# The gated output weights of a hybrid mLSTM block: preparing them beside the first q projection and the last scan

## The chip, the cores and the metric

The kernel runs on one core of a Trainium2 chip. The metric is device time in microseconds (us) of the whole program, lower is better. Engines are named as in the profile: PE (TensorE matmul) and PEld (its weight load), DVE (VectorE), ACT (ScalarE), POOL (GpSimd), and SP, whose queue issues nearly all DMAs.

## The reference, cut to what matters

One encoder layer over 2048 tokens of width 1024. `c` gives six modulation vectors, and the layer has two parts:

```python
mod = silu(c) @ w_ada + b_ada
sh1, sc1, gt1, sh2, sc2, gt2 = split(mod, 6)
h = rmsnorm(x, g_mix) * (1 + sc1) + sh1
q, k, v, o, gates, u = split(h @ w_in)
y_a = sigmoid(o) * headnorm(scan_fwd(q,k,v) + scan_bwd(q,k,v))   # 4 heads, chunks of 128 tokens
y_b = pool(u) ...                                                # windows 2, 4, 8, 16
x = x + gt1 * (concat(y_a, y_b) @ w_out)
x = x + gt2 * (square(relu(h2 @ w_ff1)) @ w_ff2)                 # h2 from x, g_ffn, sh2, sc2
return rmsnorm(x, g_final)
```

`gt1 * (y @ w_out)` is computed as `y @ (w_out * gt1)`, gt1 scaling the columns of `w_out`. That product, and every later one, is made with seven half-size products in place of eight (a Strassen form), so the scaled weight is needed as four blocks and as sums of blocks.

## The kernel before, in words

All matrix work is in split 32-bit form: an operand is a high part (an ACT copy) and a low part (a DVE subtraction), and each product takes three matmuls.

The stages, in program order:

- Norm and the v and gate projections. Beside them DVE forms columns of `mod` (`mod_col`, L119 to L123): 512 KB of `w_ada` are loaded and one L117 multiplies by silu(c) (`c_bc`) and sums, one column of 128 values each.
- Pooling, groups 3 to 0: the u projection of a group, its window sums on DVE, its part of the output weights (`wo_d`) and ten or so more columns of `mod`. The last columns, 38 to 47, come in group 0.
- `qk_proj(0)`: the k blocks 3, 2, 1, 0 of head 0 and then its q blocks 0 to 3, 512 tokens and 24 matmuls each. After each k block `k_post` transposes it, scales it twice on DVE (`kb` L497, `kf` L498) and builds four states of the backward scan (PE L508, DVE L511 and L513).
- For each head the `scan` over 16 chunks, with the `qk_proj` of the next head as *fill* between its steps (after the last head the four `o_proj`). A head later than 0 has its q blocks first and its k blocks last. The fill of head h+1 first loads `wr(h+1)` and `wr(4+h+1)` (`col_weights`, L390 to L397), turns each into `wh` (ACT L395) and `wl` (DVE L396), and then multiplies (L404 to L406).
- The output product with the scaled `w_out`, and the MLP.

**Preparing the output weights.** `mod` is transposed on PE (`modT`, L694), copied by ACT (L696), written to DRAM (`mod_d`, L697), and its row gt1 is read back on all partitions (L699). The generator `out_sums` (L666 to L684) then takes four pairs of rows, k = 0 to 3. For each it loads two 512 KB rows (`os`, L671) from `w_out` and `wo_d`, multiplies each by gt1 (L674), stores three blocks (L678), makes four block differences in place (L682), and stores each (L684). A block is 256 KB. One k is eight steps of the generator: loads, two products, the stores, four differences.

**Buffers.** The tag `raw` has three buffers of 512 KB. The loads of `w_ada`, the loads `wr` of all projections and the rows `os` share it. gt1 takes the one buffer of tag `bc`, which was `c_bc`'s. `wh` and `wl` have two buffers each. The two PSUM tiles of tag `tp` serve every transpose; the three of `ev` serve the copies of q and k, `kf`, and the copy of modT.

**What sets the order.** Up to the output product, a planner writes each engine's instruction list at build time. It follows its own estimate of when operands are ready; of the instructions that are ready in that estimate the earliest in program order goes first. A tile whose tag has no free buffer waits, in program order, until the last reader of an older tile of the tag is done. Each engine, and SP's DMA queue, then executes its list in order and waits in place. `keep_in_program_order` puts an instruction behind the one that precedes it on its engine in program order.

Of the kernel before, what the change touches and what calls it, by code (L numbers as in the profile page):

```python
# [12 lines left out]
ALU = mybir.AluOpType  # L13
# [8 lines left out]
NB = T // 512  # L22
H = 4
# [12 lines left out]
def block_kernel(ctx, tc, x, x_t, cb, w_ada, b_ada, g_mix, g_ffn, g_head, p_scale, w_col, w_vg,  # L36
                 w_v2, w_o, w_1, w_2, w_pool, b_gate, edge, g_fin, out):
    nc = tc.nc
    ve, sc, gp, pe, dma = nc.vector, nc.scalar, nc.gpsimd, nc.tensor, nc.sync.dma_start
# [16 lines left out]
    def raw(name, n=D):  # L56
        t = wp.tile([P, D], F32, tag="raw", name=name, bufs=3)
        return t[:, :n]

    def evt(name):  # L60
        return wev.tile([P, 528], F32, tag="ev", name=name)
# [4 lines left out]
    def tp(name):  # L66
        return psA.tile([P, 512], F32, tag="tp", name=name)
# [322 lines left out]
    def col_weights(ci):  # L390
        r = raw(f"wr{ci}").rearrange("p (k n) -> p k n", k=KT)
        dma(r, w_col[ci])
        hh = wq.tile([P, KT, P], F32R, tag="whi", name=f"wh{ci}")
        hl = wq.tile([P, KT, P], F32R, tag="wlo", name=f"wl{ci}")
        sc.copy(hh, r)  # L395
        ve.tensor_tensor(hl, r, asf(hh), ALU.subtract)  # L396
        return hh, hl  # L397

    def col_mm(ci, b, w):

        hh, hl = w
        ps = mm(f"c{ci}_{b}")
        for k in range(KT):
            pe.matmul(ps, hh[:, k], Hh[b][:, k], start=k == 0, stop=False)  # L404
            pe.matmul(ps, hh[:, k], Hl[b][:, k], start=False, stop=False)  # L405
            pe.matmul(ps, hl[:, k], Hh[b][:, k], start=False, stop=k == KT - 1)  # L406
            if k in (2, 5, 7):
                yield
        return ps

    def mod_row(j0):
        return mod_d[j0:j0 + KT, :].rearrange("(o a) n -> o (a n)", o=1).broadcast_to([P, D])


    with tc.tile_pool(name="pu", bufs=2) as pu, tc.tile_pool(name="psU", bufs=2, space=PSUM) as psU:
# [8 lines left out]
        for g in (3, 2, 1, 0):  # L424
# [21 lines left out]
            n = T + 15  # L446
# [30 lines left out]
    with tc.tile_pool(name="ps_", bufs=2) as sp, tc.tile_pool(name="psS", bufs=1, space=PSUM) as psS:  # L477

        def qk_proj(h, C):


            def k_post(b, ps):
                vt = sp.tile([P, 4, 129], F32, tag="va", name=f"va{h}_{b}", bufs=2)
                dma(vt, v_d[b][h])
                e = evt(f"k{h}_{b}")[:, :512]
                sc.copy(e, ps)
                dma(qk_d[h][b][:, 1, :], e)
                yield
                pt = tp(f"kn{h}_{b}")
                for j in range(4):  # L490
                    pe.transpose(pt[:, j * P:(j + 1) * P], e[:, j * P:(j + 1) * P], ident)
                pt = pt.rearrange("p (c e) -> p c e", c=4)
                r0 = h * NT + 4 * b
                kf = evt(f"kf{h}_{b}")[:, :512].rearrange("p (c e) -> p c e", c=4)
                kb = sp.tile([P, 4, P], F32, tag="kb", name=f"kb{h}_{b}", bufs=1)
                r1 = r0 + 64
                ve.tensor_tensor(kb, pt, wkcol[:, r1:r1 + 4].unsqueeze(2).broadcast_to([P, 4, P]), ALU.mult)  # L497
                ve.tensor_tensor(kf, pt, wkcol[:, r0:r0 + 4].unsqueeze(2).broadcast_to([P, 4, P]), ALU.mult)  # L498
                dma(kw_d[h][b], kf)
                yield  # L500
                for j0 in (3, 1):
                    kv = psS.tile([P, 2, 256], F32, tag="kv", name=f"kvb{h}_{4 * b + j0}")
                    for j in (j0, j0 - 1):
                        c = 4 * b + j
                        if c == 0:
                            break
                        kvj = kv[:, j0 - j, 0:129]
                        pe.matmul(kvj, kb[:, j], vt[:, j], start=True, stop=True)  # L508
                        Cn = sp.tile([P, 129], F32, tag="Cb", name=f"Cb{h}_{c}", bufs=17)
                        if c == NT - 1:  # L510
                            ve.tensor_copy(Cn, kvj)  # L511
                        else:
                            ve.scalar_tensor_tensor(Cn, C[c], decb[:, r1 + j:r1 + j + 1], kvj,  # L513
                                                    ALU.mult, ALU.add)
                        C[c - 1] = Cn
                    yield

            def q_post(b, ps):
                e = evt(f"q{h}_{b}")[:, :512]
                sc.mul(e, ps, float(P) ** -0.5)  # L520
                dma(qk_d[h][b][:, 0, :], e)


            p = iter(())
            if h == 0:
                wk_, wq_ = wn, col_weights(0)
            else:
                wq_, wk_ = col_weights(h), col_weights(4 + h)
            for n in range(2 * NB):
                is_k = (n < NB) == (h == 0)  # L530
                b = NB - 1 - n % NB if is_k else n % NB
                g = col_mm(4 + h if is_k else h, b, wk_ if is_k else wq_)
                while True:
                    try:
                        next(g)
                    except StopIteration as e:
                        ps = e.value
                        break
                    next(p, None)
                    yield  # L540
                for _ in p:
                    pass
                if is_k:
                    p = k_post(b, ps)
                    next(p)
                else:
                    q_post(b, ps)
            for _ in p:
                yield
# [108 lines left out]
        def o_proj(h):  # L658
            w = col_weights(8 + h)
            for b in range(NB):  # L660
                ps = yield from col_mm(8 + h, b, w)
                e = evt(f"o{h}_{b}")[:, :512]
                sc.copy(e, ps)
                dma_act(o_d[b][:, h, :], e)

        def out_sums(gt1):  # L666

            for k in range(4):
                rows = [raw(f"os{h}_{k}") for h in range(2)]
                for h, src in enumerate((w_o[k], wo_d[k])):  # L670
                    dma(rows[h], src)  # L671
                yield
                for h in range(2):
                    ve.tensor_tensor(rows[h], rows[h], gt1, ALU.mult)  # L674
                    yield
                b11, b12, b21, b22 = [r[:, 512 * n:512 * n + 512] for r in rows for n in range(2)]
                for place, b in ((0, b11), (1, b21), (5, b22)):
                    dma(wot_d[place, :, k], b)  # L678
                yield
                for place, dst, x_, y_ in ((3, b11, b12, b11), (4, b12, b22, b12), (2, b22, b22, b11),  # L680
                                           (6, b21, b21, b22)):
                    ve.tensor_tensor(dst, x_, y_, ALU.subtract)  # L682
                    yield
                    dma(wot_d[place, :, k], dst)  # L684

        def chain(*gs):
            for g in gs:
                yield from g

        Cb = [None] * NT  # L690
        for _ in qk_proj(0, Cb):
            pass
        mt = tp("modT")
        pe.transpose(mt[0:48, 0:P], mod, ident)  # L694
        me = evt("modTe")
# [2 lines left out]
        gt1 = wp.tile([P, D], F32, tag="bc", name="gt1", bufs=1)  # L698
        dma(gt1, mod_row(16))  # L699
        osum = out_sums(gt1)  # L700
        for h in range(H):
            Cn = [None] * NT
            if h + 1 < H:
                fill = qk_proj(h + 1, Cn)
            else:
                fill = chain(*(o_proj(i) for i in range(H)))
            n = 0
            for _ in scan(h, Cb):
                n += 1
                if n % EVERY == 0:  # L710
                    next(fill, None)
                if h > 0 and n % 4 == 0:
                    next(osum, None)
            for _ in fill:
                pass
            Cb = Cn
# [554 lines left out]
```

## Time and profile before

| what | value |
|---|---|
| time, median of 3 runs | 2049.32 us (2046.41 to 2052.79) |
| the profiled execution's own time | 2054.1 us |
| its span, first to last instruction | 2052.2 us |
| mean granted TensorE clock | 0.996 of full speed |
| busy: PE, PEld, DVE, ACT, POOL | 97%, 81%, 66%, 45%, 6% of the span |

The 2052.2 us are the stretch that the views show; 1.9 us of the execution lie outside it. "Busy" counts an instruction from its start to its modelled end, so PE is busy at 97% and still has room in places; the idle time of PEld is the sharper sign. In this execution the q blocks of head 0 run from about 268 us to 291 us, the scan of head 0 with the fill of head 1 to about 375 us, those of heads 1 and 2 to about 455 and 537 us, and the last scan to about 605 us.

### The profile page before, as it was taken

The numbers are of one execution on the slowest core, as the hardware profiler recorded it, in microseconds if no ns is written. First come the engines' busy times: TensorE is split into PE (matmuls) and PEld (weight loads), VectorE is DVE, ScalarE is ACT, GpSimd is POOL, SyncE is SP. The second block draws the span as 40 slices with busy tenths as digits, with TensorE's granted clock in tenths as the row PEclk, the third lists the DMA queues.
The fourth block names the chain that finished last, engine by engine and source line by source line (L and its number), as shares of the span: only waits on it lengthen the run. The fifth ranks groups of instructions, "written<-read, shape, count | busy, mean of one in ns | idle before, by whom it ended". The sixth has DMA issues, their size and how long they took to land.

```text
span 2052.2 us, 27784 instructions
## 1 busy us (share of the span) xinstructions
PE 1991.4 (97%) x9591; PEld 1659.4 (81%) x9591; DVE 1356.0 (66%) x2456; ACT 917.9 (45%) x1704; POOL 132.0 (6%) x353
## 2 busy tenths in 40 slices
PE   7999998989999999999999999999999999999998
PEld 6887777778887877788888888888888888888886
DVE  6638646666646766555666766666877767767876
ACT  4722123333335667655556755556323324324432
POOL 1100012222210110000000000000000000000011
PEclk9999999999999999999999999999999999999999
DMA  8836866877548798655666766666877748658554
GB/s 340 232 114 216 275 198 214 255 254 225 176 141 269 234 276 282 199 185 188 196 218 209 257 217 210 216 213 219 303 258 247 239 153 257 227 156 274 191 165 132
DMA packets 298574, 452.87 MB, mean 221 GB/s; under 512 B 23569, under 2 KB 163137, under 8 KB 298306
## 3 DMA queue, kind: packets, MB, share of 16 engines
q1 hardware_dynamic: 228546, 413.35, 62.0%
q10 hardware_dynamic: 69888, 37.76, 6.0%
q8 instruction: 75, 1.23, 0.2%
q14 instruction: 65, 0.53, 0.1%
HBM read 290.40 MB, written 160.62 MB: 220 GB/s over the span
## 4 chain that ended last, share of the span: by engine, by line
PE 74%; DMA 7%; DVE 4%; ACT 1%; issue 1%; SPq 1%; POOL 1%; POOLq 0%; DVEq 0%; ACTq 0%
PE c L406 3%; PE c L405 3%; PE c L404 3%; DMA ua<-uad 2%; DMA ada<-in_w_ada 1%; DMA os<-in_w_o 1%; PE g313x L845 1%; PE g312x L845 1%; PE g311x L845 1%; PE g310x L845 1%; PE g303x L845 1%; PE g302x L845 1%; PE g301x L845 1%; PE g300x L845 1%; PE g213x L845 1%
## 5 line engine op out<-in xcount | busy, mean ns | idle before, releaser
L404 PE MATMUL c<-Hh,wh 128*128 128x512 f32 x512 | 211.0, 412 | 1.1 <-ACT wh L395 1.1
L406 PE MATMUL c<-Hh,wl 128*128 128x512 f32 x512 | 202.9, 396 | 0.5 <-DVE wl L396 0.5
L405 PE MATMUL c<-Hl,wh 128*128 128x512 f32 x512 | 203.3, 397 | 0.0
L406 PEld LDWEIGHTS c<-Hh,wl 128*128 128x128 f32 x512 | 96.6, 189 | 20.6 <-DVE wl L396 1.0
L404 PEld LDWEIGHTS c<-Hh,wh 128*128 128x128 f32 x512 | 97.0, 189 | 18.7 <-ACT wh L395 1.6
L405 PEld LDWEIGHTS c<-Hl,wh 128*128 128x128 f32 x512 | 97.0, 189 | 16.8 <-issue 0.7
L581 ACT ACTIVATE ua<-ua,vcol 128x128 f32<-128x128 f32 x64 | 25.7, 401 | 106.8 <-POOL ua L577 106.8
L117 DVE SCALAR_TENSOR_TENSOR ada<-ada,c_bc 128x1024 f32<-128x1024 f32 x48 | 58.0, 1220 | 22.7 <-DMA ada<-in_w_ada 22.6
L961 POOL TENSOR_TENSOR g300ss<-g300ss 128x1 f32<-128x1 f32 x2 | 0.9, 451 | 1085.4 <-ACT g300j L957 1085.4
L780 ACT CAST wb<-rwb 128x1024 fp32r<-128x1024 f32 x56 | 58.7, 1050 | 24.9 <-DMA rwb<-twd 24.8
L783 DVE TENSOR_TENSOR wb<-rwb,wb 128x1024 fp32r<-128x1024 f32 x56 | 68.2, 1218 | 0.5 <-ACT wb L780 0.5
L622 ACT ACTIVATE jk<-hm 128x128 bf16<-128x128 f32 x64 | 19.7, 307 | 83.7 <-DVE hm L620 83.1
L586 DVE TENSOR_TENSOR ua<-ua,q 128x256 f32<-128x256 f32 x64 | 26.5, 426 | 38.5 <-DMA ua<-uad 26.6
L577 POOL TENSOR_SCALAR_AFFINE_SELECT ua<-ua 128x128 f32<-128x128 f32 x64 | 26.2, 410 | 275.0 <-DMA ua<-uad 172.3
L625 DVE TENSOR_TENSOR hm<-hm,hss 128x256 f32<-128x256 f32 x32 | 14.6, 457 | 39.0 <-POOL hss L129 39.0
L255 PE MATMUL vgp<-vgh,Hh 128*128 128x272 f32 x128 | 37.5, 296 | 2.3 <-ACT Hh L208 2.3
L440 ACT COPY u<-c 128x512 f32<-128x512 f32 x16 | 9.4, 586 | 62.6 <-PE c L406 62.6
L257 PE MATMUL vgp<-vgl,Hh 128*128 128x272 f32 x128 | 36.9, 290 | 0.4 <-DVE vgl L229 0.4
L256 PE MATMUL v2p<-v2h,Hh 128*128 128x256 f32 x128 | 35.9, 283 | 1.2 <-ACT v2h L236 1.2
L783 DVE TENSOR_TENSOR ob<-rob,ob 128x1024 fp32r<-128x1024 f32 x14 | 17.1, 1224 | 30.1 <-ACT ob L780 29.5
L259 PE MATMUL vgp<-vgh,Hl 128*128 128x272 f32 x128 | 36.7, 291 | 0.0
L585 DVE TENSOR_TENSOR ua<-ua,S 128x256 f32<-128x256 f32 x64 | 26.5, 414 | 14.6 <-PE S L584 14.2
(4048 smaller groups left out, 6079.0 us busy)
## 6 DMA issues: line engine op xcount, KB each, us to landing
rwb<-twd SPq DMA_DIRECT2D x56, 512.0 KB, 6.0
ada<-in_w_ada SPq DMA_DIRECT2D x48, 512.0 KB, 4.9
ua<-uad SPq DMA_DIRECT2D x64, 256.0 KB, 4.1
j<-in_w SPq DMA_DIRECT2D x32, 512.0 KB, 5.3
twd<-t SPq DMA_DIRECT2D x64, 256.0 KB, 3.0
twd<-j SPq DMA_DIRECT2D x48, 256.0 KB, 2.7
wr<-in_w_col SPq DMA_DIRECT2D x16, 512.0 KB, 5.1
q<-qkd SPq DMA_DIRECT2D x32, 256.0 KB, 3.6
```

The lines of the kernel that those rows point to most:

```text
L117: ve.scalar_tensor_tensor(w, w, 1.0, c_bc, ALU.mult, ALU.mult, accum_out=mod[:, j:j + 1])
L255: pe.matmul(pa[:, :VG], hh, vgh[k], start=st, stop=False)
L256: pe.matmul(pb[:, :256], hh, v2h[k], start=st, stop=False)
L257: pe.matmul(pa[:, :VG], hh, vgl[k], start=False, stop=False)
L259: pe.matmul(pa[:, :VG], hl, vgh[k], start=False, stop=en)
L404: pe.matmul(ps, hh[:, k], Hh[b][:, k], start=k == 0, stop=False)
L405: pe.matmul(ps, hh[:, k], Hl[b][:, k], start=False, stop=False)
L406: pe.matmul(ps, hl[:, k], Hh[b][:, k], start=False, stop=k == KT - 1)
L585: ve.tensor_tensor(W, W, S[:, 0:P].unsqueeze(1).broadcast_to([P, 2, P]), ALU.mult)
L780: sc.copy(dst, src)
L783: ve.tensor_tensor(dst, src, asf(hi), ALU.subtract)
L845: pe.matmul(ps, a[:, k], b[:, k], start=start and k == 0 and n == 0, stop=k == 3 and n == 2, skip_group_check=not start)
```

## The change

The transpose of `mod`, its store, the load of gt1 and the creation of `out_sums` move ahead of `qk_proj(0)`. The steps of `out_sums` no longer run in every fourth step of scans 1 to 3. The first step (the loads of k = 0) is taken in the last k block of head 0; two steps follow each of the twelve steps of its q blocks, that is k = 0, 1, 2 in full and the loads of k = 3; the other steps of k = 3 run in every fourth step of the last scan. The products by gt1 are pinned to program order on DVE.

```diff
                 for h in range(2):
-                    ve.tensor_tensor(rows[h], rows[h], gt1, ALU.mult)
+                    tc.keep_in_program_order(ve.tensor_tensor(rows[h], rows[h], gt1, ALU.mult))
                     yield
...
         Cb = [None] * NT
-        for _ in qk_proj(0, Cb):
-            pass
         mt = tp("modT")
         pe.transpose(mt[0:48, 0:P], mod, ident)
...
         osum = out_sums(gt1)
+
+        for n, _ in enumerate(qk_proj(0, Cb)):
+            if n == 3 * NB - 3:
+                next(osum)
+            elif n >= 3 * NB:
+                for _ in range(2):
+                    next(osum)
         for h in range(H):
...
-                if h > 0 and n % 4 == 0:
+                if h == H - 1 and n % 4 == 0:
                     next(osum, None)
```

## Rows read from the trace of the kernel before

**Rows 1.** Windows: stretch, its length, PE, PEld, DVE, ACT, POOL busy, clock, DMA.
```profile
262.00:290.00 28.00, 27.81 (x135) 22.59 (x136) 8.56 (x19) 5.74 (x13) 1.18 (x5) 1.00 0.57 188
290.00:375.00 85.00, 77.55 (x449) 64.63 (x447) 54.66 (x166) 27.19 (x84) 19.68 (x48) 1.00 0.70 219
...
537.00:605.00 68.00, 68.00 (x400) 59.22 (x400) 38.59 (x137) 24.33 (x75) 15.83 (x40) 1.00 0.47 141
```
**Rows 2.** Waits of PEld, 290 to 375: total us, times, longest.
```profile
PEld kn L491 <- ACT k L486: 2.4, 2, 2.0
...
PEld hT L632 <- PE kn L491: 1.1, 1, 1.1
...
PEld kvf L602 <- DVE Cb L513: 0.6, 2, 0.4
```
**Rows 3.** Waits of PEld, 375 to 537.
```profile
PEld kvb L508 <- DVE Cf L607: 3.6, 3, 2.0
...
PEld S L584 <- DVE ua L585: 0.2, 1, 0.2
```
**Rows 4.** Waits of SP's queue, 240 to 480.
```profile
SPq L671 <- DMA wotd<-os: 6.7, 3, 3.0
...
SPq L392 <- DMA wotd<-os: 6.2, 3, 2.6
```
**Rows 5.** Timeline of SP's queue.
```profile
249.57 1.25 SPq L392 DMA_DIRECT2D wr<-in_w_col  x2
252.62 0.33 SPq L484 DMA_DIRECT2D va<-vd  x1
...
294.58 0.50 SPq L671 DMA_DIRECT2D os<-in_w_o  x1
...
329.50 0.38 SPq L671 DMA_DIRECT2D os<-wod  x1
```
**Rows 6.** Timeline of DVE.
```profile
248.95 0.16 DVE L123 TENSOR_TENSOR mod<-mod,bada 128x1 f32<-128x1 f32 x1
...
270.90 0.68 DVE L498 TENSOR_TENSOR kf<-kn,wkcol 128x512 f32<-128x512 f32 x1
```
**Rows 7.** Groups by line, whole span: busy us, mean ns.
```profile
L585 DVE TENSOR_TENSOR ua<-ua,S 128x256 f32<-128x256 f32 x64 | 26.5, 414 | 14.6 <-PE S L584 14.2
...
L674 DVE TENSOR_TENSOR os<-os,gt 128x1024 f32<-128x1024 f32 x8 | 9.8, 1223 | 7.3 <-DMA os<-wod 4.5 <-DMA os<-in_w_o 2.4 <-DMA gt<-modd 0.5
...
L612 DVE SCALAR_TENSOR_TENSOR den<-n,den 128x2 f32<-128x2 f32 x64 | 9.7, 152 | 0.3
...
L682 DVE TENSOR_TENSOR os<-os 128x512 f32<-128x512 f32 x8 | 5.5, 692 | 3.3 <-DMA wotd<-os 3.3
```
**Rows 8.** Landing times: lines L671, L678, L684, tile wr (240 to 300), tile modd.
```profile
DMA to landing us min/median/max: 4.3/5.1/7.4
...
DMA to landing us min/median/max: 2.2/3.3/4.6
...
DMA to landing us min/median/max: 2.4/4.4/5.5
...
DMA to landing us min/median/max: 4.5/4.9/6.0
...
DMA to landing us min/median/max: 3.3/6.4/7.5
```
**Rows 9.** Timelines of PE, PEld and ACT.
```profile
290.87 0.48 PE L404 MATMUL c<-Hh,wh 128*128 128x512 f32 x1
...
256.49 0.30 PEld L508 LDWEIGHTS kvb<-va,kb 128*128 128x128 f32 x2 [1.85 <-issue]
...
279.99 0.60 ACT L520 ACTIVATE q<-c 128x512 f32<-128x512 f32 x1 [5.17 <-PE c L406]
285.38 0.60 ACT L520 ACTIVATE q<-c 128x512 f32<-128x512 f32 x1 [4.79 <-PE c L406]
290.59 1.05 ACT L395 CAST wh<-wr 128x1024 fp32r<-128x1024 f32 x1 [4.62 <-PE c L405]
```

## The prediction, made before the changed kernel was run

> **What bounds the kernel now.** I read the page first, then the windows of the stretches around the change, then the waits of PE's weight loads and of SP's queue, then the timelines. The reader should see three things.
>
> PE bounds. In the q blocks of head 0 (262 to 290) PE is busy 27.8 of 28.0 us and DVE only 8.6, while in the scan of head 0 (290 to 375) DVE works 54.7 of 85.0 us and PE loses time [rows 1]. So the work that moves goes from a stretch where DVE is short to one where it is free.
>
> In the scan of head 0 the weight loads wait 11.8 us in eight groups, of which the largest, the fifth and the last are shown. Two of them (2.4 + 1.1) do not wait for DVE; the other six, 8.3 us, do [rows 2]. In scans 1 and 2 six groups wait for DVE, 9.2 us in sum, first and last shown [rows 3]. That is all that taking DVE work out of scans 0 to 2 can give: 17.5 us. Though program order has `out_sums` only from scan 1 on, the planner runs its first loads from 294.58 [rows 5], so scan 0 has its share of it.
>
> The three `raw` buffers are a chain of their own. `wr1` and `wr5` are loaded at 249.57, forty us before the fill of head 1 needs the first, because two `raw` buffers are free by then. The second row of k = 0 is loaded only at 329.50, 35 us after the first [rows 5], and on SP's queue loads of `os` and of `wr` stand 6.7 and 6.2 us behind stores of `os` that have not landed [rows 4]. So rows and projection weights really do hand the same buffers to each other.
>
> **The transpose of mod moved forward.** The last column of `mod` is done at 249.1 [rows 6]. Transpose, copy, store and load follow: store landing 3.3 us, load of gt1 some 6.4 [rows 8], so gt1 stands by about 262. The first product is pinned behind `kf` of k block 0, which ends at 271.6 [rows 6]: gt1 costs no wait there. Two things may cost. SP holds its queue until the store has landed, 3.3 us, and behind it come the loads `va` (252.62) [rows 5], for which the weight loads have already lost 1.85 us at 256.49 [rows 9]. And PE may meet the transpose before `mod` is done. The trace has no row for either. Below, a gain of 1 us (the same hold-up goes from the start of scan 0); above, 5 us: the 3.3 and the 1.85 once more. I take +1, nearer the lower end, since a few other issues usually fit into such a hold.
>
> **The steps of k = 0, 1, 2 beside the q blocks.** On DVE they are 6 products of 1.22 and 12 differences of 0.69 [rows 7], 15.6 us. DVE has 19 us free from 262 to 290 [rows 1], so its own time is covered. The DMAs are not. Each k loads two rows and stores seven blocks, and the next rows need its buffers. I follow the chain with the median landings: load 5.1, first stores 3.3, last stores 4.4 [rows 8], 0.35 an issue.
>
> - At 249.57 the two free buffers now go to `os` of k = 0, ahead of `wr1` and `wr5` in program order; the third, when `wr0` is converted, to the first row of k = 1.
> - k = 0: the products run from 271.6 to 274.1. The first block's store has landed at 272.8 + 0.35 + 3.3 = 276.5, two differences (1.4) and the store of the second (0.35 + 4.4) free the first row at 282.6.
> - k = 1: its second row loads then. Load 5.1, product 1.2, two differences 1.4, store 4.75: the first buffer is free at 295.1.
> - k = 2: its second row loads at 295.1. Load 5.1, product 1.2, three store issues 1.05 and landing 3.3, two differences 1.4, store 4.75: 16.8 us, its second row is free at 311.9. The rows of k = 3 take the two buffers that came free before that and, as their products stand in the last scan, keep them until then.
> - `wr1` is therefore the next to get a buffer, at 311.9. It lands 4.9 us later [rows 8], ACT converts it in 1.05 [rows 9]: the fill of head 1 can start at about 318. Before, its first matmul was at 290.87 [rows 9].
>
> With the shortest landings of the same rows it is 308, with the longest 330. From then on the weights of heads 1 to 3 pass through one buffer, but each is wanted some 40 us after the last, so that costs nothing; if that cover went, a load would show at 4.9 us.
>
> **What the hole costs.** From 291 to 318 PE has only the scan. The stage's PE work is 85.0 − 11.8 = 73.2 us [rows 1, 2]. Of it eight blocks at 285.38 − 279.99 = 5.4 us [rows 9] are 43.2, fifteen pairs of backward products at 0.30 [rows 9] 4.5; 25.5 are left for 16 chunks and a few transposes, so I take 1.5 us a chunk. How many chunks go by? On DVE a chunk costs 2.58 us (nine groups of rows, the largest and the smallest shown, the one with 32 instructions at half) [rows 7], and 8 us of the 27 go to the differences of k = 1 and all of k = 2: at most 7. At the pace of before, 16 in 85 us, it would be 5. I take 6, 9 us of PE work. The stage then ends at 318 + (73.2 − 9) + 3.5, the two waits that are not DVE's, = 385.7 instead of 375: +10.7 us. At 308 it is +0.7; at 330, with 7 chunks, +21.2.
>
> **What comes back.** Scans 1 and 2 lose their share of the 9.2 us [rows 3]; some of these waits are the chain of states itself, so +0 to −9.2, and I take −5. That scan 0 has no DVE waits left is in the sum above already.
>
> **k = 3 in the last scan.** There DVE is busy 38.6 of 68.0 us and PE without a gap [rows 1]; two products and four differences, 5.2 us, fit. A pinned product may hold a state up; at the rate of before (17.5 us for 24 DVE instructions) it would be 4. So 0 to 4; I take 1, nearer the covered end.
>
> **Sum.** +10.7 − 5 + 1 + 1 = +7.7 us on the profiled execution's 2054.1. That execution lies 4.8 above the median of the runs, so I put the difference on the median: 2049.3 + 7.7 = 2057.
>
> The Trainium skill ("DMA: Bandwidth & Descriptors", on the anatomy of one DMA) gives a DMA 2.0 us plus bytes over 436 GB/s. As an estimate from that page a row would land in 3.2 us and a block in 2.6, where the trace has 5.1 and 3.3 to 4.4 [rows 8]; the page's chain ends at 306 and its stage is no longer than before, which would make the whole about 3 us faster, inside the resolution. The measured landings decide.
>
> **Rivals.**
>
> *Faster.* If `wr1` is loaded before the rows of `os`, or these pass their buffers on by 291, there is no hole and the stage loses its 8.3 us behind DVE: −8.3 − 5 + 2 = −11, 2038 us. For it speaks that DVE has 19 us free exactly there; against it that three rounds of load, store and store must pass in 20 us, with 16.8 the sum of one round. By the sum above the fill must be able to start before about 304 to show as faster. The Trainium skill ("Perfetto Trace Analysis", on optimization strategy) says that stretches bound by different engines may gain from being interleaved; by it alone the time would be this one.
>
> *No change.* The chain runs near its shortest landings, the fill starts near 308, and +0.7 − 5 + 2 leaves −2: 2047 us.
>
> *Slower still.* The planner fixed PE's order with shorter DMAs than the chip has, so that PE's list comes to the fill before `wr1` is there and the scan stands behind it. Then the 9 us of chunks are not done in the hole: +16.7, 2066 us. For it: the existing waits of SP behind stores [rows 4] are of this kind. Against: PE waits of before are 2 us at most [rows 2, 3].
>
> **How the numbers follow.** The forecast has 0.44; its own bounds put it from 2045 to 2073, so about a quarter of it lies within 0.3% (6.1 us, about what a measurement of this kernel can tell from no change). Faster has 0.24, no change 0.18, slower still 0.14. That makes slower by over 0.3%: 0.34 + 0.14 = 0.48; within: 0.10 + 0.18 = 0.28; faster 0.24. The range of 8 in 10 reaches from the middle of the faster case, 2038, to past the slower one, 2074; half of the faster case (0.12) is left out below, some 0.05 above.
>
> **What the new profile would show.** Right: the `os` loads of k = 0 near 250 where the `wr` loads stood; `wr1` issued long after 291, behind a store of `os`; first matmul of the fill of head 1 between 308 and 330 while scan chunks go on; PE busy clearly under 0.9 from 291 to 320; scans 1 and 2 shorter by some 2 to 3 us each. Wrong: `wr1` loaded near 250 as now, or the fill starting at 291. The number would also fail if the transpose of `mod` stopped PE or SP for more than 5 us between 249 and 260.

## The result, and the profile after

The changed kernel took 2062.6 us (median of 6 runs, 2058.7 to 2066.4) against 2049.6 for the kernel before (6 runs, 2045.5 to 2052.9) on the same chip: a ratio of 1.0056, 95% interval 1.0038 to 1.0075. It is slower by 13 us as the medians stand. The profiled execution has a span of 2060.1 us and a time of 2061.9.

Windows of the changed kernel (stretch, length, busy time of PE, PEld, DVE, ACT, POOL, granted clock, DMA share, GB/s):

```profile
262.00:290.00 28.00, 28.00 (x139) 22.73 (x138) 16.43 (x30) 5.06 (x12) 2.15 (x8) 1.00 0.80 254
290.00:305.00 15.00, 8.23 (x41) 7.31 (x39) 10.60 (x30) 1.40 (x5) 0.14 (x1) 0.74 0.90 293
305.00:318.00 13.00, 6.80 (x23) 4.88 (x22) 4.99 (x16) 2.68 (x7) 2.03 (x5) 0.50 0.80 258
290.00:375.00 85.00, 71.68 (x375) 60.52 (x374) 47.06 (x142) 23.31 (x68) 15.84 (x38) 0.86 0.66 211
537.00:605.00 68.00, 62.64 (x363) 54.13 (x362) 40.71 (x137) 21.72 (x70) 16.26 (x42) 0.97 0.62 192
```

Against [rows 1]: beside the q blocks DVE rose from 8.6 to 16.4 us and PE stayed full, so the cover that the change looks for is there. Behind them PE is busy 15.0 of 28 us (290 to 318), and the last scan, which had no gap, has one of 5 us.

SP's queue in the changed kernel, some of the loads of `os` rows (L671), of projection weights (L392) and of `ua` (L569), which holds what a chunk of the scan starts from; the first `os` row went out at 244.32:

```profile
250.10 0.41 SPq L671 DMA_DIRECT2D os<-wod  x1
...
281.27 0.41 SPq L671 DMA_DIRECT2D os<-wod  x1
...
294.45 0.40 SPq L671 DMA_DIRECT2D os<-wod  x1
297.90 0.33 SPq L671 DMA_DIRECT2D os<-in_w_o  x1
...
309.59 0.38 SPq L671 DMA_DIRECT2D os<-wod  x1
...
312.10 0.33 SPq L392 DMA_DIRECT2D wr<-in_w_col  x1
312.48 0.90 SPq L569 DMA_DIRECT2D ua<-uad  x2
```

Where [rows 5] have both `wr` loads at 249.57, this queue has `os`; `wr1` goes out at 312.10, behind the last row of k = 3, after a wait of 1.5 us on the queue for a store of `os`. The `ua` loads of the next chunks stand behind it and land from 317.5 on.

What follows on ACT, and PE's order around it:

```profile
316.31 1.04 ACT L395 CAST wh<-wr 128x1024 fp32r<-128x1024 f32 x1 [2.59 <-DMA wr<-in_w_col]
```
```profile
295.52 0.80 PE L584 MATMUL S<-q 128*128 128x128 f32 x2 [4.12 <-DVE ua L585]
...
304.42 0.77 PE L595 MATMUL n<-v,ua 128*128 128x129 f32 x2 [2.18 <-DVE den L611]
...
312.52 0.47 PE L632 MATMUL hT<-ident,hm 128*128 128x128 f32 x1 [3.24 <-DVE hm L625]
...
317.41 0.80 PE L404 MATMUL c<-Hh,wh 128*128 128x512 f32 x1 [1.46 <-ACT wh L395]
318.00 0.63 PE L405 MATMUL c<-Hl,wh 128*128 128x512 f32 x1
...
321.02 0.40 PE L404 MATMUL c<-Hh,wh 128*128 128x512 f32 x1
321.25 0.39 PE L405 MATMUL c<-Hl,wh 128*128 128x512 f32 x1
```

The fill of head 1, at 290.87 before [rows 9], begins at 317.41. In the hole between there is only the scan, in small groups with waits of 2 to 4 us between them.

DVE in that hole, the ends of chunks (L620; first and last of four) and some of the moved steps:

```profile
273.03 2.35 DVE L674 TENSOR_TENSOR os<-os,gt 128x1024 f32<-128x1024 f32 x2
...
300.68 0.35 DVE L620 SCALAR_TENSOR_TENSOR hm<-n,den,hm 128x128 f32<-128x128 f32 x1
...
301.33 1.22 DVE L674 TENSOR_TENSOR os<-os,gt 128x1024 f32<-128x1024 f32 x1
...
310.09 0.35 DVE L620 SCALAR_TENSOR_TENSOR hm<-n,den,hm 128x128 f32<-128x128 f32 x1
```

**A ledger.** To put the 13 us in places I cut the executions at ACT's copies: the last q block of head 0 (A), the last k block of heads 1, 2 and 3 (B, C, D; a scan with its fill lies between two of them), and the last block of the output projection (E). For the changed kernel A, B and E are

```profile
291.04 0.60 ACT L520 ACTIVATE q<-c 128x512 f32<-128x512 f32 x1 [4.90 <-PE c L406]
...
385.37 0.57 ACT L486 COPY k<-c 128x512 f32<-128x512 f32 x1
...
655.32 0.59 ACT L663 COPY o<-c 128x512 f32<-128x512 f32 x1 [0.16 <-PE c L406]
```

"Fill" is the first q copy of head 1, counted from A. Kernels 3 to 14 are the experiments below, one profiled execution each; the same kernel profiled twice (rows e5 and g4) differs by up to 2.5 us in A to E, so less than that means little. A set is the DVE work of one k: two products and four differences.

| kernel | fill | scan 0 (A–B) | scan 1 (B–C) | scan 2 (C–D) | last (D–E) | A–E |
|---|---|---|---|---|---|---|
| before | 10.3 | 80.6 | 81.8 | 75.8 | 112.9 | 351.1 |
| changed | 35.4 | 94.3 | 76.2 | 75.0 | 118.8 | 364.3 |
| e3_wr_first | 11.7 | 82.7 | 75.0 | 75.5 | 118.6 | 351.8 |
| e2_k3_late | 21.6 | 85.0 | 75.9 | 75.3 | 115.7 | 352.0 |
| e4_no_pin | 24.4 | 88.2 | 76.1 | 75.7 | 113.0 | 353.0 |
| e5_front_only | 9.0 | 76.7 | 80.1 | 75.0 | 113.7 | 345.5 |
| f1_k3_scan0 | 9.8 | 81.6 | 76.0 | 75.1 | 112.7 | 345.4 |
| f2_k3_tail | 11.8 | 78.4 | 75.1 | 74.5 | 117.4 | 345.4 |
| f3_k0_only | 8.5 | 71.8 | 80.4 | 80.9 | 112.7 | 345.7 |
| f4_pin_only | 10.9 | 73.4 | 82.9 | 82.7 | 114.3 | 353.3 |
| g1_chunk_act | 44.1 | 98.6 | 76.1 | 74.6 | 118.6 | 367.9 |
| g2_k0_no_pin | 8.6 | 75.9 | 77.8 | 74.2 | 113.5 | 341.3 |
| g3_k3_scan0_no_pin | 7.7 | 83.5 | 75.8 | 75.0 | 113.5 | 347.9 |
| g4_front_again | 8.5 | 76.5 | 82.3 | 76.2 | 113.0 | 348.0 |

The changed kernel: +13.8 in scan 0, −6.5 in scans 1 and 2, +6.0 in the last scan, +13.2 together, and +1.0 ahead of A (from the conversion of `wr4`, the weights of head 0's k blocks, to A 58.2 us, before 57.2). That is 14.2, for the 13 of the medians. The spans of the two profiled executions differ by only 7.9, since in the one of before the stretch after E was 4.7 us longer, and that ahead of this conversion 1.5; nothing of the change lies there. The same stretch ahead of A is 58.9 to 60.6 us in the six kernels below that ask for the weights first (e3, f1, f2, f3, g2, g3), 1.7 to 3.4 us longer than before, which counts against what the table shows for them from A to E. One us of it means little: f4, whose program is that of before up to A, has 57.9.

### The profile page after: what moved, and what is told of

The parts are those of the page before. It is cut to its first block, busy times and chain, and to the rows that moved or that the text cites. A ratio compares the mean times of both kernels' runs of the same rounds, so it can differ in the third digit from the quotient of the medians.

```text
span 2060.1 us, 27802 instructions
## 1 busy us (share of the span) xinstructions
PE 1995.0 (97%) x9591; PEld 1664.9 (81%) x9591; DVE 1359.6 (66%) x2456; ACT 918.8 (45%) x1704; POOL 133.6 (6%) x353
## 4 chain that ended last, share of the span: by engine, by line
PE 76%; DMA 6%; DVE 5%; ACT 1%; issue 1%; POOL 1%; SPq 0%; DVEq 0%; POOLq 0%; ACTq 0%
PE c L405 3%; PE c L406 3%; PE c L404 3%; DMA ua<-uad 2%; PE S L584 1%; PE n L598 1%; PE n L595 1%; PE n L597 1%; PE n L600 1%; PE kvf L602 1%; PE f101x L850 1%; PE g313x L850 1%; PE g312x L850 1%; PE g311x L850 1%; PE g310x L850 1%
## 5 line engine op out<-in xcount | busy, mean ns | idle before, releaser
L406 PEld LDWEIGHTS c<-Hh,wl 128*128 128x128 f32 x512 | 97.4, 190 | 21.1 <-DVE wl L396 1.4
```

## The experiments

The theory after the result: the rows of k = 0 to 3, asked for ahead of `wr1`, hold the three `raw` buffers, and the hole in PE until `wr1` comes is the loss. The rivals: (a) the moved steps cost by contention, on DVE, on the DMA engines and on SP's queue, wherever `wr1` stands; (b) the early transposition is the cost; (c) the pin on the products is. All edits are against the changed kernel unless another is named.

**The weights first (e3_wr_first).** Both weights of head 1 are asked for at the first step of the q projection, ahead of the `os` rows.

```diff
         for n, _ in enumerate(qk_proj(0, Cb)):
+            if n == 0:
+                first = col_weights(1), col_weights(5)
...
-                wq_, wk_ = col_weights(h), col_weights(4 + h)
+                wq_, wk_ = first if h == 1 else (col_weights(h), col_weights(4 + h))
```

> The two weights of head 1 (wr1, wr5) are asked for ahead of the rows of the output weights, everything else is as in the changed kernel. Buffer theory (the three raw buffers go to the rows first, so wr1 waits for the store of k = 2): wr1 loads near 250 and the fill of head 1 starts at 291 instead of 317; k = 1 and 2 then run beside scan 0 and cost part of what they did before, so about 2050 us (2046 to 2055). Rival, contention (the six products and their stores on DVE and on SP's queue hold up the scan itself, and the late fill only goes with it): same DVE and DMA work in the same place of the program, so it stays within 3 us of 2062.6.

2053.6 against 2053.5 for the kernel before on that chip: 1.0003 [0.9991, 1.0015]. The expectation of the buffer theory is met. On SP, and the fill's first product on PE:

```profile
246.71 2.25 SPq L392 DMA_DIRECT2D wr<-in_w_col  x2
253.78 0.57 SPq L392 DMA_DIRECT2D wr<-in_w_col  x1
258.86 0.82 SPq L671 DMA_DIRECT2D os<-in_w_o  x1
```
```profile
295.92 0.47 PE L404 MATMUL c<-Hh,wh 128*128 128x512 f32 x1
```

A is at 296.69 here, so the fill starts 0.8 us ahead of A; in the kernel before it was 0.7 (290.87 and 291.55). The hole is gone, and with it 11.7 of the 13.8 us of scan 0. So the order in which the buffers are asked for is the cause of the hole, and the hole of most of the loss. Two things are left: scan 0 is 5.9 us longer than where only the transposition moved (e5), and the last scan still loses 5.7.

**k = 3 late (e2_k3_late).** The generator is stopped ahead of k = 3, whose rows are asked for, in program order, in the last scan; the planner puts their loads at 418.0 and 454.9.

```diff
             elif n >= 3 * NB:
-                for _ in range(2):
+                for _ in range(1 + (n < 6 * NB - 1)):
                     next(osum)
```

> The two loads of k = 3 are taken in the last scan instead of at the end of the q blocks; nothing else moves. Buffer theory: wr1 gets the buffer that the first row of k = 3 took at 297.9 instead of the one at 312.1, so the fill starts near 303 instead of 317, and about 10 us come back: 2052 us (2049 to 2056). Contention theory: two loads of 512 KB less of 14 beside scan 0, at most 1 or 2 us: 2060 to 2063.

1.0001 [0.9989, 1.0012]. `wr1` follows the rows of k = 2 directly:

```profile
295.22 0.40 SPq L671 DMA_DIRECT2D os<-wod  x1
...
299.15 0.33 SPq L392 DMA_DIRECT2D wr<-in_w_col  x1
```

13 us earlier than in the changed kernel, the fill at 306.7 instead of 317.4, scan 0 shorter by 9.3. So the rows of k = 3 do take buffers ahead of `wr1`, as the prediction had it.

**Without the pin (e4_no_pin).**

```diff
-                    tc.keep_in_program_order(ve.tensor_tensor(rows[h], rows[h], gt1, ALU.mult))
+                    ve.tensor_tensor(rows[h], rows[h], gt1, ALU.mult)
```

> The products by gt1 are no longer pinned to program order on DVE. Buffer theory: gt1 stands by 258, so the first products can run up to 13 us before 273, the chain of rows and stores ends that much earlier, wr1 loads near 300 and the fill starts near 305: 2053 us (2049 to 2058), if the earlier products don't hold up the states of the k blocks. Contention theory: the same work, now also between the k blocks' steps: 2062 or more.

1.0026 [1.0013, 1.0038]. The planner now takes the products earlier, the first at 257.6 instead of 273.0 and k = 3's in scan 0 too; `wr1` goes out at 301.3, scan 0 is 88.2 us, and the last scan, which has no step left, is at 113.0. The fill begins at 310.5, not near 305 as the buffer theory expected. About half of the loss goes with the pin (1.0056 to 1.0026): its share here is that it starts the chain of buffers later, and that it keeps k = 3 in the last scan.

**The transposition alone (e5_front_only, g4_front_again).** The kernel before with `modT`, `modd` and `gt1` ahead of the projection, and nothing else; on two chips.

```diff
         Cb = [None] * NT
-        for _ in qk_proj(0, Cb):
-            pass
         mt = tp("modT")
...
         osum = out_sums(gt1)
+        for _ in qk_proj(0, Cb):
+            pass
```

> Only the transpose of mod, its store and the load of gt1 are moved ahead of the first projection; the steps of the output weights stand in scans 1 to 3 as in the kernel before, without the pin. Both theories: PE waits some 2.4 us for the last column of mod and gets about as much back, so within 2 us of before: 2048 to 2052. A third theory, that the early transpose and SP's wait for its store are what costs: 2055 to 2060.

> The kernel that moves only the transposition and the load of gt1, once more, beside the three others on one chip: 0.9977 of the kernel before in its first comparison, so 2045 to 2047 if that holds.

0.9977 [0.9963, 0.9990], and 0.9982 [0.9970, 0.9994]. Rival (b) falls: this part makes the kernel faster, by about 4 us, where the first expectation had it give back only what it costs. Ahead of A it takes 1.0 to 1.3 us more than before, and from A to E 3.1 to 5.6 less. The weight loads of the second of these kernels between 288 and 375:

```profile
PEld kvb L508 <- DVE Cf L607: 3.0, 3, 1.5
...
PEld kn L491 <- ACT k L486: 0.4, 1, 0.4
```

All its waits there come to 7.8 us, where before they were 11.8 [rows 2]; among the lost ones is the 2.0 us for ACT's copy of a k block. Which of the issues at the start of scan 0 (store of `modTe`, load of `gt1`, ACT's copy) had caused these waits was not separated.

**k = 3 in scan 0 (f1_k3_scan0) and behind the last scan's loop (f2_k3_tail).** Both have the weights first.

```diff
-                if h == H - 1 and n % 4 == 0:
+                if h == 0 and n % 4 == 0:
                     next(osum, None)
```
```diff
+                for _ in range(1 + (n < 6 * NB - 1)):
...
             for _ in fill:
-                pass
+                if h == H - 1:
+                    next(osum, None)
```

> The weights wr1 and wr5 asked for ahead of the os rows, and the steps of k = 3 in the scan of head 0 instead of the last one; k = 0 to 2 stay beside the q blocks. If the 5 to 6 us that the last scan lost in the changed kernel (118.8 against 112.9 us up to the last copy of the tail) come from k = 3's products and differences in it, this stage comes back to 113 to 114 us, and the time to some 2048 to 2050, if the scan of head 0 takes four more DVE pairs without a new wait (82.7 us in the kernel with the weights first). Rival: the last scan is slow because its own order of instructions came out differently, whatever k = 3 does; then it stays at 118 and the time at 2053.

> The weights first, the rows of k = 3 loaded in the last scan as in the kernel that delays them, and its products and differences behind the last scan's loop, in what is left of the output projection. If the pinned products in the scan's chain of states cost the 5 us, the last stage falls to about 113 us. Rival: it is the late store of the block sums that the output projection waits for; then moving them still later makes the stage longer, over 119 us, and the time 2054 or more.

f1: 0.9995 [0.9982, 1.0007]; f2: 0.9993 [0.9980, 1.0005]. With k = 3 out of it, f1's last stage is 112.7 us, that of before, and scan 0 does not grow against e3 (81.6 and 82.7), which loads the same two rows there; f2, which has neither these loads nor these steps in scan 0, takes 78.4. Weight loads of the changed kernel from 525 to 662, and then windows of the changed kernel and of f1:

```profile
PEld hT L632 <- DVE hm L625: 4.2, 1, 4.2
```
```profile
545.00:565.00 20.00, 16.02 (x94) 14.08 (x93) 13.00 (x44) 4.89 (x18) 4.27 (x12) 0.91 0.65 202
```
```profile
545.00:565.00 20.00, 20.00 (x120) 17.51 (x119) 11.81 (x40) 8.70 (x26) 5.75 (x16) 1.00 0.56 180
```

So 4 us of PE in one place, beside k = 3's two products and its stores. The chain of that wait can be read in the changed kernel on SP's queue (with the landing of its `ua` load at 550.70), on POOL and on DVE:

```profile
548.25 0.86 SPq L678 DMA_DIRECT2D wotd<-os  x2
...
550.70 0.48 SPq L569 DMA_DIRECT2D ua<-uad  x1
551.27 0.38 SPq L678 DMA_DIRECT2D wotd<-os  x1
```
```profile
DMA to landing us min/median/max: 5.7/5.7/5.7
```
```profile
556.52 0.29 POOL L577 TENSOR_SCALAR_AFFINE_SELECT ua<-ua 128x128 f32<-128x128 f32 x1 [3.93 <-DMA ua<-uad]
```
```profile
546.61 1.22 DVE L674 TENSOR_TENSOR os<-os,gt 128x1024 f32<-128x1024 f32 x1
...
549.55 1.22 DVE L674 TENSOR_TENSOR os<-os,gt 128x1024 f32<-128x1024 f32 x1
...
558.13 0.42 DVE L625 TENSOR_TENSOR hm<-hm,hss 128x256 f32<-128x256 f32 x1 [4.32 <-POOL hss L129]
```

POOL waits until 556.52 for the `ua` load of 550.70; its `hss` stands behind that, DVE's `hm` behind `hss`, and PE's transpose of `hm` behind it. The same load and its landing times in this stage in f1:

```profile
535.09 1.95 SPq L569 DMA_DIRECT2D ua<-uad  x2
```
```profile
DMA to landing us min/median/max: 3.2/3.6/4.0
```

In f1 the two loads go out 9.6 and 11.1 us after D (525.55), in the changed kernel 10.4 and 14.2 us after it (536.50), the second behind two of the products' stores, and it needs 5.7 us to land. SP did not stand still for the products: these end at 547.8 and 550.8, and each of their stores goes out right behind the issue before it. So the load was 3.1 us late in going out and some 2 us late in landing. That the stores are the whole of it was not tried by itself; that k = 3 is, f1 shows. In f2 the planner still ran the products at 562, inside the scan; its last stage is 117.4 with other waits (3.5 us at `n` for `Cf`). The rival given there, a store that the output projection waits for, is not what the trace shows.

**Only k = 0 beside the q blocks (f3_k0_only, g2_k0_no_pin).** Weights first, k = 1 to 3 in scans 1 to 3, with and without the pin.

```diff
-            elif n >= 3 * NB:
-                for _ in range(2):
+            elif n >= 3 * NB and n < 3 * NB + 4:
+                for _ in range(1 + (n < 3 * NB + 3)):
                     next(osum)
...
-                if h == H - 1 and n % 4 == 0:
+                if h > 0 and n % 4 == 0:
```

> The weights first, only k = 0 beside the q blocks, k = 1 to 3 at every fourth chunk of the scans of heads 1 to 3 as before, products pinned. If the passing of three buffers between rows and weights in the scan of head 0 is the cost, this has none of it: the scan of head 0 at 77 to 80 us, as in the kernel that moves only the transposition (76.7), scans 1 and 2 at 155 together, the last one at 113; 2045 to 2049 in all. If mixing any of these steps with the q blocks costs by itself, the scan of head 0 stays near 82 and the time over 2051.

> The kernel with the weights first and only k = 0 beside the q blocks, without the pin on the products. The pin alone cost 4.9 us against the kernel before. If it costs in scans 1 and 2 because the product is held behind chunk work and its rows then hold the buffers, this kernel's scans of heads 1 and 2 fall from 161 us to 155 to 157, and the time to 2043 to 2045. Rival: with k = 0 out of the way the pin costs nothing more, and it stays at 2049 like the pinned one.

f3: 0.9988 [0.9977, 0.9999]; g2: 0.9978 [0.9966, 0.9990], at 2048.0 us and not the 2043 to 2045 of its first expectation. f3 came out as the buffer theory has it in scan 0, which has no product or difference and is the shortest of all, 71.8 us; but scans 1 and 2, which hold three sets of two products and four differences, are 161.3 together, against 151 where they hold none (f1). That is 3 to 4 us a set, of 5.2 us of DVE by [rows 7]. Without the pin (g2) k = 1 and 2 move to scan 0 and k = 3 to scan 1, which take 75.9 and 77.8: some 2 us a set. So the sets cost wherever in the scans they lie, more with the pin: rival (a) is right for this remainder, though not for the hole. Neither theory had expected that the sets would cost in later scans what they save in scan 0.

**The pin on the kernel before (f4_pin_only).**

```diff
-                    ve.tensor_tensor(rows[h], rows[h], gt1, ALU.mult)
+                    tc.keep_in_program_order(ve.tensor_tensor(rows[h], rows[h], gt1, ALU.mult))
```

> The kernel before with the products kept in program order and nothing else. If the pin by itself costs nothing, 2049 within 3 us. Rival: a pinned product holds DVE's order in the scans up, as the comparison of the changed kernel with and without it leaves open (2062.6 against 2058.0): then 2052 to 2055.

1.0024 [1.0012, 1.0037], +4.9 us. Pinned, the products stand in scans 1, 2 and 3 (the last set at 536.9), scan 0, which had two sets before, becomes 7.1 us shorter, and scans 1 and 2 together 7.9 longer, the last 1.5. So rival (c) is right for the kernel before. In the two pairs here that have the weights first and k = 0 beside the q blocks (f3 and g2, f1 and g3), pinned and unpinned differ by less than the intervals.

**Chunk loads of head 0 on ACT's queue (g1_chunk_act).**

```diff
+            ld = dma_act if h == 0 else dma
...
-                    dma(q2, qk_d[h][b][:, :, sl])
+                    ld(q2, qk_d[h][b][:, :, sl])
```

and the same for `w2`, `v2` and `ua`.

> The changed kernel, with the chunk loads of head 0's scan (q2, w2, v2, ua) issued on ACT's queue instead of SP's; rows of os and projection weights as they are. In the changed kernel only four chunks went by while PE had no fill work, since the chunk loads stood on SP behind a load of os that waited for a store. If that is what kept the hole empty, six or more chunks are done in it, with the fill still starting between 312 and 318 us (the buffers are the same), and the scan of head 0 takes about 91 us instead of 94.3: 2059 in all. Rival: what the chunks lack in the hole is DVE, busy with the differences and the chain of states; then four or five chunks go by and the time stays at 2062.

1.0106 [1.0092, 1.0119]: 2074.5 us, 22 more than before. The expectation missed the time altogether. The window of its hole, and then on DVE, SP and PE the second product of k = 2, the end of the fourth chunk, `wr1` and the start of the fill:

```profile
297.50:333.00 35.50, 19.65 (x102) 17.05 (x102) 21.83 (x73) 7.97 (x27) 7.26 (x18) 0.81 0.88 282
```
```profile
311.56 1.29 DVE L675 TENSOR_TENSOR os<-os,gt 128x1024 f32<-128x1024 f32 x1
...
320.46 0.34 DVE L621 SCALAR_TENSOR_TENSOR hm<-n,den,hm 128x128 f32<-128x128 f32 x1
```
```profile
327.51 0.33 SPq L392 DMA_DIRECT2D wr<-in_w_col  x1
```
```profile
333.04 0.79 PE L404 MATMUL c<-Hh,wh 128*128 128x512 f32 x1 [1.20 <-ACT wh L395]
```

Seven chunks instead of four were done in the hole, but the hole was longer too: in its first 26 us, the length of that of the changed kernel, four were done here as well. So this run does not show that the queue had kept the hole empty. And the chain of buffers got longer: counted from A (297.1 here), the second product of k = 2 stands at +14.4 instead of +10.3 (301.33 in the changed kernel), and `wr1` at +30.4 instead of +21.1. What delayed the rounds, the chunk work now between them on DVE or the fuller DMA engines (share 0.88), was not separated. Scan 0 goes with the start of the fill: with it 21.6, 24.4, 35.4 and 44.1 us after A (e2, e4, changed, g1), scan 0 took 85.0, 88.2, 94.3 and 98.6.

**Without the pin, k = 3 in scan 0 (g3_k3_scan0_no_pin).** f1 with the product as in e4.

> The kernel with the weights first, k = 0 to 2 beside the q blocks and k = 3 in the scan of head 0, without the pin. All of this work now lies in the scan of head 0, so scans 1 and 2 (151 us) and the last stage (112.7) have nothing to gain from the missing pin; the scan of head 0 (81.6 us) may lose the part of it that is the held order: 2046 if the pin costs there as in the changed kernel (4.6 us with it and without), 2050 if not.

0.9989 [0.9979, 0.9999], no different from f1.

Rows of `os` in buffers of their own, which would cut the chain instead of reordering it, were not tried.

## Why the prediction was right, and where its terms were off

The time lies in the range, 5.6 us above the value, on the side that was given the most chance. The mechanism of the main term, the hole, is the one that was forecast, and e3 and e2 show it; the terms that were off missed mostly to the same side, and the wide range took them in.

- **The front, +1.** Measured +1.0, which is no more than single executions differ by (f4 has +0.7 there without the move). PE does meet the transpose before `mod` is done:

```profile
PEld modT L692 <- DVE mod L123: 2.4, 1, 2.4
```

 What the term left out is that the stretch after A gains more than that from the move (e5, g4). In the prediction the possible gain was bounded at 1 us; it is 3.1 to 5.6 from A on in these two runs.
- **The chain of buffers.** Forecast: products from 271.6, second row of k = 1 at 282.6, of k = 2 at 295.1, `wr1` at 311.9, fill at about 318. Measured: 273.0, 281.3, 294.5, 312.1, 317.4. The step from landings and issues to the start of the fill was right. The sum by the landing figure of the Trainium skill ("DMA: Bandwidth & Descriptors", on the anatomy of one DMA) ended at 306; between the two, the measured landings were the better ones. That section fits its figure to DMAs that GpSimd issues, and these go out on SP's queue.
- **What the hole costs, +10.7.** Measured +13.8. The hole was as long as forecast, but four chunks were done in it instead of six: 2 × 1.5 = 3.0 us more to do later. After the fourth chunk, which ended at 310.4, none ended in the hole: the next `ua` loads had gone out only at 312.48, behind the `os` row and `wr1`. Whether the queue was the cause stays open, since g1, with these loads on another queue, did no more in the same time. And the fill began at half the clock: its first eight products took 3.6 us (317.41 to 321.02), the next eight 1.8, so 1.8 us more. The prediction had no term for the clock. 10.7 + 3.0 + 1.8 = 15.5, 1.7 over what was measured.
- **What comes back, −5.** Measured −6.5. 5.7 of it is in scan 1, where before the sets of k = 2 and 3 lay, and 0.9 in scan 2, which had none; the prediction had 2 to 3 in each. f3 and g2 show what a set costs in a scan.
- **k = 3 in the last scan, +1.** Measured +6.0, outside the bounds of 0 and 4. This is the worst of the terms, 5 of the 6.5 us by which the sum of the profiled terms (14.2) exceeds the forecast 7.7. The step that failed is "at the rate of before": it counted DVE's waits, and the 4.2 us came by way of a `ua` load that went out and landed late, behind the products' stores.
- **The faster rival** had as its condition that `wr1` is loaded before the rows. e3 is that kernel, and it is no faster. The 8.3 us behind DVE in scan 0 were not there to be gained, as long as the rounds of k = 1 and 2 still run into it (steps until 315); f3, with no set in scan 0, has it 8.8 us shorter than before, but scans 1 and 2, which then hold three sets, 3.6 longer. Even with the last scan's loss removed (f1) the whole is within the resolution of before. The rule of the Trainium skill ("Perfetto Trace Analysis", on optimization strategy) that interleaving stretches with different bounds may help did not decide here: DVE had the time beside the q blocks, but the buffers and the DMAs did not.
- **The no-change rival** said that a fill at 308 costs 0.7. e2's fill at 306.7 cost 4.4 in scan 0.
- **Slower still** put 2066 on PE's list coming to the fill first, with nothing done in the hole. The list did not: four chunks were done in the hole, two fewer than forecast.

What stays open: which of the issues that left the start of scan 0 gives the 4 us of e5, whether SP's queue kept chunks out of the hole, and whether all four sets could be hidden from PE: beside the q blocks PE stayed full, but three sets do not pass there in time, and each in a scan cost 2 to 4 us.

## What to carry to other kernels

When work is moved to a stretch where its engine is free, follow its buffers before its engine: here three buffers shared between two users went to the one that was first in program order, and the other then waited for whole rounds of load, work and store. Move the requests of the later user ahead by hand (here that alone took back 12 of the 14 us of the first scan), and look on each queue at the loads that come to stand behind the moved work's loads and stores: one such load was 3 us late in going out and 2 us late in landing, and PE stood for 4.2. Test the parts of such a change alone: here the small one, a transposition out of the busy stretch, gave the only gain that these runs show, and the large one none with its faults mended.

## What was not expected of the hardware

The granted clock fell when PE had little to do, and came back late. Windows of the changed kernel around the start of the fill (columns as above):

```profile
311.00:317.40 6.40, 2.29 (x6) 1.29 (x6) 0.77 (x2) 1.52 (x2) 0.89 (x2) 0.50 0.80 261
317.40:321.00 3.60, 3.59 (x8) 2.66 (x9) 2.74 (x5) 1.39 (x4) 2.64 (x6) 0.51 0.78 253
321.00:326.00 5.00, 5.00 (x23) 4.10 (x22) 1.65 (x2) 2.15 (x4) 1.80 (x3) 1.00 0.84 259
```

PE had waited 4.1 us up to 295.52, and 2.2 and 3.2 us later on. In 305 to 317.4 the clock was 0.50, the level of 1.2 GHz, and still 0.51 in 317.4 to 321, where PE is busy throughout; from 321 it was 1.00, 2.4 GHz. Products that follow one another every 0.23 us at the upper level (321.02, 321.25) came every 0.43 at the lower (318.00, 318.42). The Trainium skill ("TensorE: Matmul & The Clock Gate", on what is actually happening) says that the array runs at 1.2 GHz after idling and at 2.4 GHz when busy; the trace agrees. So a hole in PE costs more than its idle time: the scan work done in it, and the first products behind it, go at half the pace.
